# One result row per token and choice in an MoE kernel: written, not added, and summed on TensorE

## The chip, the cores and the metric

One core of a Trainium2 chip runs the whole program. The metric is device time in microseconds (us), the median of the runs shown. The engines are PE (TensorE, matmuls), DVE (VectorE), ACT (ScalarE), POOL (GpSimd) and SP (SyncE, which here issues transfers and does nothing else). "SPq" and "POOLq" in a row are the sequencers of these engines: issuing a transfer, waiting on a semaphore.

## What is computed

Two layers of a decoder step for 576 tokens of 1024 numbers (512 of a prompt, 64 of eight samples). Each layer is three kinds of sequence mixers behind one input projection, an output projection, a normalised residual, and then a mixture of 16 experts of which every token uses two, the two best of its best group of four. The part that this change touches, cut from the reference and put in short form:

```
h  = layer_norm-ed, modulated x            # [576, 1024]
e1, e2, w1, w2 = the two experts of a token, and their weights
y  = w1 * expert(e1, h) + w2 * expert(e2, h)
       # expert: silu(h @ W1) * (h @ W3) @ W2, 256 hidden
x  = layer_norm(ALPHA * x + gate * y)      # layer 0: goes on to layer 1's
                                           # projection; layer 1: the output
```

All of it is float32, and expert weights differ from layer to layer: 16 experts of three matrices of 1 MB each.

## The kernel before, in words

Tokens are five tiles of 128 rows, the fifth of 64 (the samples). The program runs through the mixers, the output projection with routing, the experts, and the combination of a layer; layer 0's combination feeds layer 1's input projection tile by tile.

**Rows.** The modulated input h of each token is stored by SP in a tensor hbuf in DRAM (L1633), one row for each token. Routing counts on the chip how many tokens each expert has and makes tables of row numbers. Blocks 0 to 15 are the experts in a fixed order; seven of the blocks (`LIGHT`) take 64 rows, the others up to 128, and further blocks stand in branches for experts with more tokens. Four left-over blocks, in a branch `nx > 0` (L2056) behind all others, are not needed with these inputs, so the branch is skipped.

**A block.** `gather` (L1314) is an indirect transfer that POOL issues: rows of hbuf by a column of the table. PE transposes them, `up` multiplies by W1 and W3 (float32 values in two parts for blocks of 128 rows), `hid` makes the hidden values, `down` multiplies by W2. ACT and DVE copy the result, times the token's weight, into a tile ys, of which there are two. `scatter` (L1379) is an indirect transfer by POOL that adds ys to rows of ybuf in DRAM. Two experts' scatters may add to the same row, so each waits until the one before it of another expert has landed; `declare_no_dep` lifts this only among the blocks of one expert. Nearly every scatter stands in the program twice, in the two sides of a branch `half` (for all rows, or for half of them), of which one is executed; `parts` returns the first of them. ybuf is zeroed in the mixers' time (L569).

**The order around it.** The loop over b is written out by hand: in its step b, PE goes from `up` of block b to `turn` of block b+1, POOL issues the gather of block b+2, then come `down` and `scatter` of block b-1. [...] SP loads the weights of three to four blocks ahead, 1 MB at a time, into three sets of buffers (wraw, slots, w3rd).

**The end of a layer.** Before the scatter of block 14, SP issues loads of ybuf for tiles 0 and 1 (`EARLY`, `take`, L1883). The results of blocks 14 and 15 reach these two tiles another way as well: `down` writes a second copy, times the gate g2 (L1368, DVE), into the tiles of gathered rows, and PE adds the right rows with a matrix of zeros and ones, `hot` (L2111, four matmuls of 128x512 for each tile). The scatters of blocks 14 and 15 are declared free of the EARLY loads, in their first variant (`st = parts(...)[0]`) and not in the second, which is the one executed here, so that one waits for these loads. Behind the branch of the left-over blocks SP loads the rows of tiles 4, 2 and 3. `combine` multiplies the rows by g2 (DVE, L2034 and L2096), adds them to x (L2098, L2122), and normalises: a reciprocal root in nine tiny DVE instructions (L353 to L359), then ACT, and the scale and shift by the rows of ln, on POOL (L2265 and L2266, or L2277 and L2284) and for the last tiles on DVE (L2279). In layer 0, a tile that is normalised is transposed by PE (L469), and layer 1's projection starts.

Of the kernel before, what the change touches and what calls it, by code (L numbers as in the profile page):

```python
# [44 lines left out]
THIRD = [b for b in range(NE) if RANK[b] < 2 + 2 * T // 257]  # L45
ORDER = (4, 0, 1, 2, 3)
# [15 lines left out]
def _tables():  # L62
# [47 lines left out]
    put("tok", np.stack([np.tile(p[:, None] - 127, (1, 5)), np.tile(128 * np.arange(5) - 896, (128, 1))], 2))  # L110

    put("off", 2046 + (p[:, None] >= 64))
# [43 lines left out]
def _body(nc, tc, a, ctx, dbg):  # L156
# [60 lines left out]
    hbuf = dp.tile([T, D], F32, name="hbuf")  # L217
    ybuf = dp.tile([T, D], F32, name="ybuf")
# [341 lines left out]
    def conv(l, S, hT, sp_):  # L560
# [6 lines left out]

        for t in ORDER:
            sp.dma_start(ybuf[tsl(t)], bz[:tp_(t)].rearrange("p g t -> p (g t)")[:, 0:D])  # L569
# [603 lines left out]
    def numbers(R, t, A):  # L1173

        n = tp_(t)
        for k in range(2):
            for i in range(2):
                dve.tensor_scalar(A[:, i, k], R["oh"][:n, t, i], R["w"][:n, t, i:i + 1] if k else R["tok"][:n, t, 0:1], None, op0=ALU.mult)
# [42 lines left out]
    def left_over(R, raw, tabs):  # L1221
# [14 lines left out]
        dve.tensor_tensor(tok[:, :, 0], *[C("tok").rearrange("p (t a) -> p t a", a=2)[:, :, i] for i in range(2)], op=ALU.add)  # L1236
# [32 lines left out]
        dve.tensor_scalar(tabs[0][:, c], ds, 1023.0, None, op0=ALU.add)  # L1269
# [29 lines left out]
    class Block:  # L1299
# [12 lines left out]
        def gather(self, r=None):  # L1312
            r = r or slice(0, self.rows)
            self.got = pool.indirect_dma_start(out=self.X[r], out_offset=None, in_=hbuf[:, :],  # L1314
                                    in_offset=bass.IndirectOffsetOnAxis(ap=self.tabs[0][r, self.col:self.col + 1], axis=0),
                                    bounds_check=T - 1, oob_is_err=False)
# [41 lines left out]
        def down(self, g=None, yg=None):  # L1358

            b, ys, wt = self.col, self.ys, self.tabs[1]  # L1360
            v = self.w[2].rearrange("p (f n) -> p f n", f=2)
            for h in range(2):
                c = slice(512 * h, 512 * (h + 1))
                p = ps(pl=self.pl)
                for f in range(2):
                    pe.matmul(p, self.hT[:, f], v[:, f, c], start=(f == 0), stop=(f == 1))  # L1366
                if yg is not None:
                    dve.scalar_tensor_tensor(yg[:, c], p, wt[:, b:b + 1], g[:, c], op0=ALU.mult, op1=ALU.mult)  # L1368
                if h == 0 or yg is not None:
                    act.activation(ys[:, c], p, AF.Copy, scale=wt[:, b:b + 1])  # L1370
                else:
                    dve.tensor_scalar(ys[:, c], p, wt[:, b:b + 1], None, op0=ALU.mult)

        def scatter(self, r=None):
            r = r or slice(0, self.rows)
            return self.add(ybuf[:, :], self.ys[r], self.to[r], T)

        def add(self, out, rows, to, n):
            st = pool.indirect_dma_start(out=out, in_=rows, in_offset=None,  # L1379
                                         out_offset=bass.IndirectOffsetOnAxis(ap=to, axis=0),  # L1380
                                         bounds_check=n - 1, oob_is_err=False, compute_op=ALU.add)
            for c, o in self.scat:
                if c % NE == self.col % NE and self.col < 3 * NE:
                    tc.declare_no_dep(st.ins, o.ins, reason="an expert's rows are distinct")
            self.scat.append((self.col, st))
            return st

    class Light(Block):
# [8 lines left out]
        def gather(self, r=None):  # L1397
            if not self.part:
                return super().gather(slice(0, 64))

            pool.indirect_dma_start(out=self.X[:, 0:512], out_offset=None, in_=hbuf[:, :].rearrange("t (h c) -> (t h) c", h=2),
                                    in_offset=bass.IndirectOffsetOnAxis(ap=self.tabs[3][:, 1, self.col:self.col + 1], axis=0),
                                    bounds_check=2 * T - 1, oob_is_err=False)
# [37 lines left out]
        def scatter(self, r=None):  # L1441
            return self.add(ybuf[:, :].rearrange("t (h c) -> (t h) c", h=2), self.ys[:, 0:512],
                            self.tabs[3][:, self.part, self.col:self.col + 1], 2 * T)
# [49 lines left out]
    def phase_b(l, gates, nrm, gst, slots, rqk, rv, x, R, tabs, rst, fill):  # L1493
# [123 lines left out]
        def experts_in(t):  # L1617
# [15 lines left out]
            sp.dma_start(hbuf[128 * t:128 * t + n], hps[t][:n].rearrange("q k p -> q (k p)"))  # L1633
# [51 lines left out]
        def ranked(t):  # L1685
# [3 lines left out]
            dve.tensor_tensor(An[:n, t, :, 0:2], bc(R["oh"][:n, t], 2, 2), bc(bc(C("tok")[:n, 2 * t:2 * t + 2], 1, 2), 3, 16), op=ALU.mult)  # L1689
# [26 lines left out]
        def finish(tq):  # L1716
# [9 lines left out]
            dve.tensor_scalar(srci[:, 0, 2:], pv[:, 0, 0, 2:], 1023.0, None, op0=ALU.add)  # L1726
            dve.tensor_scalar(srci[:, 1:3], pv[:, 1:3, 0], 1023.0, None, op0=ALU.add)
# [80 lines left out]
        dve.scalar_tensor_tensor(tabs[0][:, 0:2], pt[:, 384:386], 1023.0, tabs0, op0=ALU.add, op1=ALU.add)  # L1808
# [5 lines left out]
    def experts(last, finish, l, x, R, tabs, slots, rqk, rv, ahead):  # L1814
# [8 lines left out]
        with ExitStack() as sE:  # L1823
# [16 lines left out]
            def aside(b):  # L1840
# [10 lines left out]
                if b == NE - 2:  # L1851

                    o = _OFFS["iota256"][0]
                    src = lp.tile([128, 3, 2], F32, name="srcf", tag="ab", bufs=1)
# [3 lines left out]
                    dve.tensor_scalar(src[:, 1], src[:, 0], 256.0, 1024.0, op0=ALU.is_lt, op1=ALU.mult)  # L1858
                    dve.tensor_tensor(to, src[:, 0], src[:, 1], op=ALU.add)
                    for i in (1, 0):  # L1860
                        bl[NE - 2 + i].to = to[:ROWS[NE - 2 + i], i:i + 1]
                        dve.tensor_scalar(hot[:, 256 * i:256 * (i + 1)], hot[:, 0:256], src[:, 0, i:i + 1], None, op0=ALU.is_equal)
# [8 lines left out]
            def light(b, X, pl, part, y):  # L1871
                return Light(b, tabs, scat, X, xf[b % 2], hids[b % 2 if part == 0 else 2], y, sl if part == 0 else sl2, pl, part)
            bl = [light(b, Xs[b % 2], psp, 0, yss[b % 2]) if b in LIGHT else
                  Block(b, tabs, scat, Xs[b % 2], xs[b % 2], hids[b % 2], yss[b % 2], sl, psp, ROWS[b]) for b in range(NE)]

            gated = Xs[:2]
            hot = rv.rearrange("p t d -> p (t d)")
            bufs, loads = (slots[0][:, 0:D], slots[0][:, D:2 * D], slots[1][:, 0:D], slots[1][:, D:2 * D], slots[2][:, 0:D]), {}
            ys = dict(zip(CORDER, bufs))

            def take(t):

                loads[t] = sp.dma_start(ys[t][:tp_(t)], ybuf[tsl(t)])  # L1883
# [69 lines left out]
            for b in range(NE + 1):  # L1953
# [76 lines left out]
                if b > 0:  # L2030
                    if b == NE:
                        bl[b - 1].down(g2[:, 0], gated[1])
                        t = EARLY[0]
                        end = tc.keep_in_program_order(dve.tensor_tensor(ys[t], ys[t], g2[:, 0], op=ALU.mult))  # L2034
                    elif b == NE - 1:
                        bl[b - 1].down(g2[:, 0], gated[0])
                    else:
                        bl[b - 1].down()
# [4 lines left out]
                    if b > NE - 2:  # L2043
                        for t in EARLY:
                            tc.declare_no_dep(st.ins, loads[t].ins, reason="other rows")
# [10 lines left out]
            with tc.If(nx > 0), ExitStack() as sI:  # L2056
# [20 lines left out]
                t = EARLY[0]  # L2077
                dve.tensor_tensor(ys[t], ys[t], g2[:, 0], op=ALU.mult)
# [5 lines left out]
        return g2, ys, loads, take, gated  # L2084

    def combine(x, tail, rv, sG, leads):

        rp = mkpool(sG, "comb")
        g2, ys, loads, take, gated = tail
        hot = rv.rearrange("p t d -> p (t d)")  # L2090

        def pre(t):

            n, y = tp_(t), ys[t][:tp_(t)]
            if t != EARLY[0]:
                tc.keep_in_program_order(dve.tensor_tensor(y, y, g2[:n, int(t == 4)], op=ALU.mult))  # L2096
            if t in EARLY:
                dve.tensor_tensor(x[:, t], x[:, t], y, op=ALU.add)  # L2098

        def total(t):  # L2100

            n = tp_(t)
            xt, y = x[:n, t], ys[t][:n]
            st = rp.tile([128, 6], F32, name="cst", tag="cst", bufs=4)[:n]
            mu, var = st[:, 2:3], st[:, 3:4]
            if t in EARLY:
                bn = y[:, 0:12].rearrange("p (h a) -> p h a", h=2)
                for h in range(2):
                    c, p = slice(512 * h, 512 * (h + 1)), ps()
                    for i, r in ((1, gated[1]), (0, gated[0])):  # L2110
                        pe.matmul(p, hot[:, 256 * i + 128 * t:256 * i + 128 * (t + 1)], r[:, c], start=(i == 1), stop=(i == 0))  # L2111
                    if t == EARLY[0]:
                        dve.tensor_tensor(xt[:, c], xt[:, c], p, op=ALU.add)
                        dve.bn_stats(bn[:, h], xt[:, c])
                    else:
                        dve.scalar_tensor_tensor(xt[:, c], p, 1.0, xt[:, c], op0=ALU.mult, op1=ALU.add, accum_out=st[:, h:h + 1])
                if t == EARLY[0]:
                    dve.bn_aggr(st[:, 2:4], y[:, 0:12])
                    return st
                dve.tensor_scalar(mu, st[:, 0:1], st[:, 1:2], -1.0 / D, op0=ALU.add, op1=ALU.mult)  # L2120
            else:
                dve.scalar_tensor_tensor(xt, y, 1.0, xt, op0=ALU.mult, op1=ALU.add, accum_out=st[:, 0:1])  # L2122
                dve.tensor_scalar(mu, st[:, 0:1], -1.0 / D, None, op0=ALU.mult)  # L2123
# [17 lines left out]
        for t in CORDER:  # L2141
# [9 lines left out]
            yield t, mu, rstd, b, o, loads[CORDER[-1]]  # L2151
# [65 lines left out]
    for l in range(L):  # L2217
        with ExitStack() as sL:
# [22 lines left out]
            def norm_rows():  # L2241
                ln2 = [slots[:, D * i:D * (i + 1)] for i in (5, 0)]
# [115 lines left out]
```

## Time and profile before

| | |
|---|---|
| median of 3 runs | 1444.93 us (1441.07 to 1446.84) |
| the profiled execution | 1451.68 us, its span 1449.9 us |
| mean granted clock of PE | 0.91 |
| PE busy | 1206.7 us, 83% of the span |
| DVE, ACT, POOL busy | 830.8, 490.3, 444.5 us |
| experts of layer 0, of layer 1 | about 482 to 703 us, 1157 to 1403 us |
| POOL's transfers in all | 18.87 MB, 5.8% of 16 DMA engines |
| SP's transfers in all | 237.67 MB, 46.8% |

Times below are microseconds from the start of the span of the one execution that was profiled. In a timeline row the columns are start, duration, engine, line, operation, the tiles (out<-in), how many were joined into the row, and in brackets how long the engine was idle before it and what ended that. [...] A busy share of an engine is an average over stages with different limits, so it says little by itself; the waits do.

### The profile page before, as it was taken

The page shows a single profiled execution, that of the slowest core. Times are in us where ns is not written, and L with a number is a line of the kernel's source. Part 1 is how long each engine was busy: PE and PEld are TensorE (multiplying, and loading weights), DVE is VectorE, ACT ScalarE, POOL GpSimd, SP SyncE. Part 2 cuts the span into 40 slices and gives each one's busy share as a digit, 9 for nine tenths or more (in the row PEclk, how much of TensorE's full clock was granted, in tenths as well). Part 3 has the DMA queues.
Part 4 walks back from the last instruction along what each step waited for, and adds up shares of the span by engine and source line. Part 5 has one row for each costly group of instructions (what it writes and reads, how often), then busy time and mean ns, then how long its engine had stood idle before and what let it go on. Part 6 is the DMA issues. An engine that isn't in the chain of part 4 may idle for free. (4 is left out here: it accounts for less than half of the span.)

```text
span 1449.9 us, 22505 instructions
## 1 busy us (share of the span) xinstructions
PE 1206.7 (83%) x8086; PEld 922.8 (64%) x8086; DVE 830.8 (57%) x1903; ACT 490.3 (34%) x906; POOL 444.5 (31%) x354
## 2 busy tenths in 40 slices
PE   4999999998985688869679998999998578886980
PEld 0998677775774355557379977886676354455750
DVE  0577457446989431237786756736689833123567
ACT  0552133331343231326355313333135222222532
POOL 0014112215234553122151332232315355321215
PEclk8899999999987799969879998999998589898995
DMA  9545665855151648698444321026653173775942
GB/s 313 175 153 167 222 229 197 307 211 158 67 183 44 248 156 301 238 334 262 131 138 142 99 94 44 5 67 202 239 190 114 63 295 114 249 240 211 319 111 102
DMA packets 93135, 258.49 MB, mean 178 GB/s; under 512 B 25131, under 2 KB 53709, under 8 KB 74040
## 3 DMA queue, kind: packets, MB, share of 16 engines
q1 hardware_dynamic: 82136, 237.67, 46.8%
q0 software_dynamic: 10848, 18.87, 5.8%
q8 instruction: 86, 1.41, 0.4%
q14 instruction: 65, 0.53, 0.1%
HBM read 233.70 MB, written 34.70 MB: 185 GB/s over the span
## 5 line engine op out<-in xcount | busy, mean ns | idle before, releaser
L396 PE MATMUL ps<-whi,hT 128*128 128x256 f32 (+1 forms) x640 | 187.7, 293 | 0.8 <-DVE yi L712 0.8
L397 PE MATMUL ps<-wlo,hT 128*128 128x256 f32 (+1 forms) x640 | 182.6, 285 | 1.2 <-DVE wlo L323 1.2
L398 PE MATMUL ps<-whi,hT 128*128 128x256 f32 (+1 forms) x640 | 183.1, 286 | 0.1
L396 PEld LDWEIGHTS ps<-whi,hT 128*128 128x128 f32 (+1 forms) x640 | 116.8, 183 | 13.3 <-issue 10.3
L397 PEld LDWEIGHTS ps<-wlo,hT 128*128 128x128 f32 (+1 forms) x640 | 116.5, 182 | 4.1 <-issue 2.5
L398 PEld LDWEIGHTS ps<-whi,hT 128*128 128x128 f32 (+1 forms) x640 | 116.5, 182 | 2.3 <-issue 1.7
L386 PE MATMUL ps<-hT,whi 128*128 128x288 f32 x512 | 88.6, 295 | 0.0
L323 DVE TENSOR_TENSOR wlo<-wraw,whi 128x2048 fp32r<-128x2048 f32 x30 | 68.6, 2287 | 31.8 <-ACT whi L322 31.4
L323 DVE TENSOR_TENSOR wlo<-w3rd,whi 128x2048 fp32r<-128x2048 f32 x22 | 67.4, 3092 | 27.8 <-ACT whi L322 27.8
L1345 PE MATMUL ps<-whi,xh 128*128 128x256 f32 x384 | 62.1, 308 | 22.7 <-ACT whi L322 7.7
L1379 POOL DMA_INDIRECT ybuf<-ys,srci x20 | 32.6, 1632 | 141.0 <-DVEq L1985 36.8
L386 PEld LDWEIGHTS ps<-hT,whi 128*128 128x128 f32 x512 | 74.7, 188 | 0.4 <-ACT zdt L525 0.4
L259 PE MATMUL ada<-wada,scond 128*32 128x512 f32 x384 | 57.0, 665 | 19.4 <-DMA wada<-w_ada 19.4
L1558 PE MATMUL ps<-whi,mh 128*128 128x512 f32 (+1 forms) x160 | 68.8, 430 | 3.7 <-ACT mh L1544 3.7
L1345 PEld LDWEIGHTS ps<-whi,xh 128*128 128x128 f32 x384 | 54.5, 209 | 27.1 <-DVE xl L1333 9.0
L1560 PE MATMUL ps<-whi,ml 128*128 128x512 f32 (+1 forms) x160 | 66.5, 420 | 3.2 <-DVE ml L1545 3.2
L1366 PE MATMUL ps<-w3rd,hid 128*128 128x512 f32 x128 | 62.8, 635 | 5.5 <-ACT hid L1356 5.1
L1559 PE MATMUL ps<-wlo,mh 128*128 128x512 f32 (+1 forms) x160 | 67.3, 421 | 0.0
L1314 POOL DMA_INDIRECT qk<-hbuf,srci x32 | 33.8, 1057 | 95.5 <-PE ps L1413 43.3
L322 ACT ACTIVATE whi<-wraw 128x2048 fp32r<-128x2048 f32 x30 | 57.3, 1910 | 15.7 <-PE ps L386 7.6
L1345 PE MATMUL ps<-wlo,xh 128*128 128x256 f32 x384 | 57.0, 294 | 0.2 <-DVE wlo L323 0.2
L834 POOL TENSOR_TENSOR qh<-qx,ex 128x256 f32<-128x256 f32 x32 | 29.6, 953 | 89.4 <-issue 73.5
(544 smaller groups left out, 2864.9 us busy)
## 6 DMA issues: line engine op xcount, KB each, us to landing
wada<-w_ada SPq DMA_DIRECT2D x48, 1024.0 KB
wraw<-moe_w SPq DMA_DIRECT2D x36, 1024.0 KB
slots<-moe_w SPq DMA_DIRECT2D x30, 1024.0 KB
w3rd<-moe_w SPq DMA_DIRECT2D x30, 1024.0 KB
wraw<-w_in SPq DMA_DIRECT2D x22, 1024.0 KB
wraw<-w_out SPq DMA_DIRECT2D x8, 1024.0 KB
ybuf<-bz SPq DMA_DIRECT2D x8, 512.0 KB
slots<-ybuf SPq DMA_DIRECT2D x8, 512.0 KB
```

The source lines that it names most:

```text
L259: pe.matmul(acc[32 * q:32 * q + 32, :], sc_[:, k, :], w[:, o:o + 512], start=(k == 0), stop=(k == KD - 1))
L322: split.hi = act.activation(hi[:, :n], raw[:, :n], AF.Copy)
L323: dve.tensor_tensor(lo[:, :n], raw[:, :n], hi[:, :n].bitcast(F32), op=ALU.subtract)
L386: pe.matmul(p[:mw, :], lhs[:, k, m0:m0 + mw], rhs[:, k, 288 * h:288 * (h + 1)], start=(k == 0 and lhs is vh and rhs is hT[0]), stop=(k == ...
L396: pe.matmul(p[:n], hT[0][:, k, xs], vh[:, k, :], start=(k == 0), stop=False)
L397: pe.matmul(p[:n], hT[0][:, k, xs], vl[:, k, :], start=False, stop=False)
L398: pe.matmul(p[:n], hT[1][:, k, xs], vh[:, k, :], start=False, stop=(k == KD - 1))
L1345: pe.matmul(p, x[:, k], v[:, k], start=(x is self.xh and v is vh and k == 0), stop=(x is self.xl and k == KD - 1))
L1366: pe.matmul(p, self.hT[:, f], v[:, f, c], start=(f == 0), stop=(f == 1))
L1558: pe.matmul(p[:n], mh[:, k, :n], vh, start=(k == 0), stop=False)
L1559: pe.matmul(p[:n], mh[:, k, :n], vl, start=False, stop=False)
L1560: o = pe.matmul(p[:n], ml[:, k, :n], vh, start=False, stop=(k == 3))
```

## The change

- hbuf and ybuf have 1152 rows instead of 576: row t for a token's first choice and row 576 + t for its second. Every row of h is stored twice (L1633), and the tables hold the number of the row by choice.
- A scatter is a plain write. All scatters are declared independent of one another.
- Only tiles 0 and 1 of ybuf are zeroed, in both planes: four stores instead of five.
- Blocks 14 and 15 write their results as the other blocks do, ACT one half and DVE the other, into the tiles of gathered rows (`Xs`), which PE's `hot` matmuls read later; the gated copies (L1368) and the early product (L2034) are gone.
- A load of a tile of ybuf is two, one of each plane. Tiles 0 and 1 land in two weight buffers (wraw) that are free by then; tiles 4, 2 and 3 in slots. The rows of ln go into other places of slots in layer 0.
- `combine`: PE adds the two rows of a token with an identity matrix, and for tiles 0 and 1 the two `hot` products with them, in one accumulation per half of 512 columns: four matmuls a half instead of two for tiles 0 and 1, two instead of none for tiles 4, 2 and 3. DVE multiplies the sums by g2 from PSUM, half by half.

```diff
+PL, NONE = T, 2047
+NY = PL + T
...
-    hbuf = dp.tile([T, D], F32, name="hbuf")
-    ybuf = dp.tile([T, D], F32, name="ybuf")
+    hbuf = dp.tile([NY, D], F32, name="hbuf")
+    ybuf = dp.tile([NY, D], F32, name="ybuf")
...
-            sp.dma_start(hbuf[128 * t:128 * t + n], hps[t][:n].rearrange("q k p -> q (k p)"))
+            for o in (128 * t, PL + 128 * t):
+                sp.dma_start(hbuf[o:o + n], hps[t][:n].rearrange("q k p -> q (k p)"))
...
-        def add(self, out, rows, to, n):
+        def put(self, out, rows, to, n):
             st = pool.indirect_dma_start(out=out, in_=rows, in_offset=None,
                                          out_offset=bass.IndirectOffsetOnAxis(ap=to, axis=0),
-                                         bounds_check=n - 1, oob_is_err=False, compute_op=ALU.add)
-            for c, o in self.scat:
-                if c % NE == self.col % NE and self.col < 3 * NE:
-                    tc.declare_no_dep(st.ins, o.ins, reason="an expert's rows are distinct")
-            self.scat.append((self.col, st))
+                                         bounds_check=n - 1, oob_is_err=False)
+            for o in self.scat:
+                tc.declare_no_dep(st.ins, o.ins, reason="every choice of every token has its own row")
+            self.scat.append(st)
...
-                loads[t] = sp.dma_start(ys[t][:tp_(t)], ybuf[tsl(t)])
+                n = tp_(t)
+                if t not in ys:
+                    ys[t] = wraw.tile([128, 2048], F32, name="wraw", tag="raw").rearrange("p (k n) -> p k n", k=2)
+                loads[t] = [sp.dma_start(ys[t][:n, k], ybuf[PL * k + 128 * t:PL * k + 128 * t + n]) for k in range(2)]
...
         def pre(t):
-            n, y = tp_(t), ys[t][:tp_(t)]
-            if t != EARLY[0]:
-                tc.keep_in_program_order(dve.tensor_tensor(y, y, g2[:n, int(t == 4)], op=ALU.mult))
-            if t in EARLY:
-                dve.tensor_tensor(x[:, t], x[:, t], y, op=ALU.add)
+            n = tp_(t)
+            sums[t] = []
+            for h in range(2):
+                c, p = slice(512 * h, 512 * (h + 1)), ps()
+                rows = [(ident[:n, :n], ys[t][:n, k]) for k in range(2)]
+                if t in EARLY:
+                    rows += [(hot[:, 256 * i + 128 * t:256 * i + 128 * (t + 1)], kept[i]) for i in range(2)]
+                for i, (m, r) in enumerate(rows):
+                    pe.matmul(p[:n], m, r[:, c], start=(i == 0), stop=(i == len(rows) - 1))
+                sums[t].append(p)
...
         def total(t):
...
+            for h in range(2):
+                c = slice(512 * h, 512 * (h + 1))
+                tc.keep_in_program_order(dve.tensor_tensor(y[:, c], sums[t][h][:n], g2[:n, int(t == 4), c], op=ALU.mult))
...
-                ln2 = [slots[:, D * i:D * (i + 1)] for i in (5, 0)]
+                ln2 = [slots[:, D * i:D * (i + 1)] for i in (1, 3)]
```

The scheduler that orders each engine's instructions moves some of them with it. POOL's order at the end of the second layer's experts, before (`srcf` is the table of blocks 14 and 15, `srci` that of all blocks; L2056 is the branch of the left-over blocks):

```order
L1379 DMA ybuf<-ys_13035,srcf 576x1024
L1924 UNCONDITIONAL_BRANCH
L1924 REGISTER_ALU
L1924 COMPARE_AND_BRANCH
L1379 DMA ybuf<-ys_13036,srcf 576x1024
L1924 UNCONDITIONAL_BRANCH
L1916 TENSOR_LOAD ebi
L2056 COMPARE_AND_BRANCH
```

and in the changed kernel, from the last of the left-over blocks on:

```order
L2079 UNCONDITIONAL_BRANCH
L2061 UNCONDITIONAL_BRANCH
L2061 ISA
L2061 UNCONDITIONAL_BRANCH
L1935 REGISTER_ALU
L1935 COMPARE_AND_BRANCH
L1384 DMA ybuf<-qk,srcf 1152x1024
L1935 UNCONDITIONAL_BRANCH
L2280 TENSOR_TENSOR x<-x,ln_17069 128x1024
```

Block 15's scatter stood ahead of the branch and now stands behind it, in both layers. PE's order from block 15's `down` to the end of the program, before (L1366 is a matmul of `down`):

```order
L1366 MATMUL ps<-wraw,hid_13031 128x512 x2
L2111 MATMUL ps<-qk,v 128x512 x2
L1924 UNCONDITIONAL_BRANCH
L1916 TENSOR_LOAD ebi
L2056 COMPARE_AND_BRANCH
...
L2056 UNCONDITIONAL_BRANCH x2
L2111 MATMUL ps<-qk,v 128x512 x4
L2354 UNCONDITIONAL_BRANCH
```

and in the changed kernel (L1373 is the matmul of `down`, `cst` holds the identity, `qk` the kept results, `v` the matrices `hot`):

```order
L1373 MATMUL ps<-wraw,hid_13073 128x512 x4
L1935 UNCONDITIONAL_BRANCH
L1927 TENSOR_LOAD ebi
L2061 COMPARE_AND_BRANCH
...
L2061 UNCONDITIONAL_BRANCH x2
L2106 MATMUL ps<-wraw,cst 128x512
L2106 MATMUL ps<-qk,v 128x512 x2
L2106 MATMUL ps<-wraw,cst 128x512 x2
L2106 MATMUL ps<-slots,cst 64x512 x4
L2106 MATMUL ps<-slots,cst 128x512 x8
```

All of PE's sums now stand behind the branch: sixteen for tiles 0 and 1 in alternation of the two kinds, then four for each of tiles 4, 2 and 3. In the first layer it is the same, but the transposes of tile 0 stand between the sums of tile 4 and those of tile 2, where they stood ahead of all waits for the last loads before.

## Rows read from the trace of the kernel before

**Rows 1.** The page, 40 slices of 36 us: PE's granted clock in tenths.
```profile
PEclk8899999999987799969879998999998589898995
```

**Rows 2.** Busy time by stretches of 10 us, experts of the first layer.
```profile
core 0: us, PE busy (x) PEld busy (x) DVE busy (x) ACT busy (x) POOL busy (x), PEclk, DMA share, GB/s
620.00:630.00 10.00, 4.21 (x30) 4.00 (x28) 0.60 (x1) 0.00 (x0) 3.11 (x2) 0.84 1.02 394
630.00:640.00 10.00, 4.88 (x18) 2.44 (x18) 2.74 (x4) 2.35 (x5) 2.65 (x2) 0.57 1.00 350
```

**Rows 3.** The timeline (start, duration, idle before and what ended it), POOL, PE, ACT.
```profile
607.22 1.59 POOL L1379 DMA_INDIRECT ybuf<-ys,route  x1 [3.56 <-DMA ybuf<-ys,srci]
...
607.37 1.09 PE L1326 MATMUL ps<-cst,qk 128*128 128x128 f32 x8
...
618.36 3.68 POOL L1379 DMA_INDIRECT ybuf<-ys,route  x1 [9.55 <-ACTq L1974]
622.34 1.07 POOL L1314 DMA_INDIRECT qk<-hbuf,srci  x1 [0.30 <-issue]
...
634.38 0.69 ACT L1370 ACTIVATE ys<-ps,wslot 128x512 f32<-128x512 f32 x1 [17.05 <-DMA qk<-hbuf,srci]
...
635.12 1.97 PE L1326 MATMUL ps<-cst,qk 128*128 128x128 f32 x8 [10.90 <-ACT ys L1370]
```

**Rows 4.** Line L1379 from 607 us, then line L1314 from 622 us.
```profile
L1379 POOLq EVENT_SEMAPHORE  x1: 10583/10583/10583, 607.1 to 607.1; - x1
...
DMA to landing us min/median/max: 11.0/11.0/11.0
```

**Rows 5.** The waits of PE, 1160 to 1420 us (total, times, longest).
```profile
PE ps L1438 <- ACT ys L1370: 10.8, 1, 10.8
PE ps L1345 <- ACT whi L322: 4.9, 1, 4.9
PE ps L1326 <- DMA v<-hbuf,srci: 3.2, 1, 3.2
```

**Rows 6.** The timeline of POOL, the first gather of the first layer.
```profile
472.88 1.18 POOL L1314 DMA_INDIRECT qk<-hbuf,srci  x1 [6.74 <-DVE route L1143]
```

**Rows 7.** The timeline, the end of the second layer.
```profile
1397.79 16.85 SPq L1883 DMA_DIRECT2D slots<-ybuf  x5
...
1402.45 3.60 PE L2111 MATMUL ps<-qk,v 128*128 128x512 f32 x8
...
1403.20 1.43 POOL L1379 DMA_INDIRECT ybuf<-ys,srcf  x1 [9.90 <-ACT ys L1370]
...
1407.94 1.42 POOL L1379 DMA_INDIRECT ybuf<-ys,srcf  x1 [3.31 <-DMA ybuf<-ys,srcf]
...
1415.73 2.34 POOL L2284 TENSOR_TENSOR x<-x,ln 128x1024 f32<-128x1024 f32 x1
...
1416.83 2.32 DVE L2096 TENSOR_TENSOR slots<-slots 64x1024 f32<-64x1024 f32 x1 [1.71 <-DMA slots<-ybuf]
...
1422.38 1.22 DVE L2096 TENSOR_TENSOR slots<-slots 128x1024 f32<-128x1024 f32 x1
...
1424.96 2.10 DVE L358 SCALAR_TENSOR_TENSOR rq<-rq 64x1 f32<-64x1 f32 x1
```

**Rows 8.** The timeline, the end of the first layer's experts.
```profile
723.44 0.22 DVE L358 SCALAR_TENSOR_TENSOR rq<-rq 128x1 f32<-128x1 f32 x1
723.56 2.33 POOL L2265 TENSOR_TENSOR x<-x,slots 128x1024 f32<-128x1024 f32 x1 [11.94 <-ACT slots L2124]
...
723.70 2.22 DVE L359 SCALAR_TENSOR_TENSOR rq<-rq 128x1 f32<-128x1 f32 x1
...
725.95 2.38 DVE L358 SCALAR_TENSOR_TENSOR rq<-rq 128x1 f32<-128x1 f32 x1
...
730.10 1.97 PE L469 MATMUL ps<-cst,x 128*128 128x128 f32 x8 [16.59 <-ACT x L2257]
```

**Rows 9.** The groups by line, DVE: count | busy us, mean ns | idle before.
```profile
L1368 DVE SCALAR_TENSOR_TENSOR qk<-ps,wslot,slots 128x512 f32<-128x512 f32 x8 | 6.0, 748 | 6.3 <-PE ps L1366 6.3
```

More of the change, by code (lines that the diff above doesn't have):

```diff
@@ L108, in _tables @@
     put("pow2", np.tile(2.0 ** np.arange(16), (128, 1)))
-    put("tok", np.stack([np.tile(p[:, None] - 127, (1, 5)), np.tile(128 * np.arange(5) - 896, (128, 1))], 2))
-    put("off", 2046 + (p[:, None] >= 64))
+    rows = np.stack([np.tile((p - 127)[:, None, None], (1, 5, 2)),
+                     np.tile((128 * np.arange(5)[:, None] + PL * np.arange(2) + 127 - NONE)[None], (128, 1, 1))], 3)
+    put("tok", rows)
+    put("off", 2 * NONE + (p[:, None] >= 64))
     put("iota384", np.tile(np.arange(384.0), (128, 1)))
@@ L566, in conv @@
         pool.memset(bz, 0.0)
-        for t in ORDER:
-            sp.dma_start(ybuf[tsl(t)], bz[:tp_(t)].rearrange("p g t -> p (g t)")[:, 0:D])
+        for t in EARLY:
+            for k in range(2):
+                o = PL * k + 128 * t
+                sp.dma_start(ybuf[o:o + 128], bz.rearrange("p g t -> p (g t)")[:, 0:D])
         cw = cp_.tile([128, 6, 5], F32, name="cw")
@@ L1235, in left_over @@
         tok = R["tok"] = tl(NT, 2)
-        dve.tensor_tensor(tok[:, :, 0], *[C("tok").rearrange("p (t a) -> p t a", a=2)[:, :, i] for i in range(2)], op=ALU.add)
+        dve.tensor_tensor(tok, *[C("tok").rearrange("p (t k a) -> p t k a", k=2, a=2)[:, :, :, i] for i in range(2)], op=ALU.add)
         for t in ORDER:
@@ L2030, in experts @@
                 if b > 0:
[L2031 to L2038, printed above, removed]
+                    bl[b - 1].down()
                     if b == NE - 1:
@@ L2044, in experts @@
                         for t in EARLY:
-                            tc.declare_no_dep(st.ins, loads[t].ins, reason="other rows")
+                            for o in loads[t]:
+                                tc.declare_no_dep(st.ins, o.ins, reason="other rows")
                 if b == 0:
@@ L2083, in experts @@
                     take(t)
[L2084 removed]
+        return g2, ys, loads, kept
     def combine(x, tail, rv, sG, leads):
         rp = mkpool(sG, "comb")
[L2089 removed]
+        g2, ys, loads, kept = tail
         hot = rv.rearrange("p t d -> p (t d)")
+        sums = {}
         def pre(t):
[L2094 to L2098 removed]
+            n = tp_(t)
[8 more added lines that the diff above has]
+                sums[t].append(p)
@@ L2100, in total @@
         def total(t):
             n = tp_(t)
-            xt, y = x[:n, t], ys[t][:n]
+            xt, y = x[:n, t], ys[t][:n, 0]
             st = rp.tile([128, 6], F32, name="cst", tag="cst", bufs=4)[:n]
             mu, var = st[:, 2:3], st[:, 3:4]
[L2106 to L2116, printed above, removed]
-                if t == EARLY[0]:
[L2118 to L2123, printed above, removed]
@@ L2150, in combine @@
                 next(ahead, None)
-            yield t, mu, rstd, b, o, loads[CORDER[-1]]
+            yield t, mu, rstd, b, o, loads[CORDER[-1]][-1]
     def feat_ab(l, tp):
```

56 lines of the change are left out of this document (31 added, 25 removed).

## The prediction, made before the changed kernel ran

> **What bounds the kernel now.** I read the page's 40 slices first, then the waits of PE, then the timeline around the longest wait, and last the timeline at the end. [...]
>
> The longest wait of the first layer's experts is 10.90 us, from 624.2 to 635.1 us [rows 3]. Read it backwards. PE waits for ACT's ys, and ACT, idle for 17.05 us, for a gather of rows from hbuf. That gather left at 622.34 and landed 11.0 us later [rows 3, 4], at 633.3. It stood on POOL behind the scatter of 618.36, and this one behind a semaphore for 10.58 us [rows 4], from 607.1 to 617.7: the landing of the scatter of 607.22. It is the wait that adding into shared rows needs. Meanwhile the DMA engines were full, a share of 1.00 to 1.02 at 350 to 394 GB/s [rows 2].
>
> In the second layer PE's long waits are 10.8, 4.9 and 3.2 us [rows 5]. The end behind its last matmul is serial [rows 7]: scatter, landing, scatter, landing, the branch of the left-over blocks, the loads of tiles 4, 2 and 3, and then DVE from 1416.83 to the end.
>
> **The change part by part.** The profiled execution took 1451.68 us (span 1449.9); the median of the three runs is 1444.93. The sum is made against the execution, and the difference is then taken from the median.
>
> 1. Scatters write and are independent. Without the semaphore, the scatter of 618.36 can follow the one of 607.22 once that has been issued, at 607.22 + 1.59 = 608.8. The gather comes 622.34 - 618.36 = 4.0 us later, at 612.8, and lands at 612.8 + 11.0 = 623.8. ACT ran 1.0 us after the landing (634.38 against 633.3) and PE 0.7 after that, so PE goes on at 625.6 instead of 635.1: **-9.5**. Bounds: 0, if the landing grows by as much as the wait shrinks, and -10.9, the whole wait. I take -9.5, since the landing of 11.0 was already measured under full DMA engines. What is late next is a split of weights on ACT, which follows the same ys and moves with it.
>
> 2. The clock behind that wait. The same eight transposes take 1.97 us after it and 1.09 us before it [rows 3], and the clock of 630 to 640 was 0.57 with PE busy for 4.88 us [rows 2]. Without the idle time this stretch costs 4.88 x 0.57 = 2.8 us: **-2**; bounds 0 and -2.1.
>
> 3. The second layer's experts. The 10.8 us are a ys buffer that its own scatter has not left yet; a plain write must land too before the buffer is rewritten, so nothing is won. The 3.2 us wait is for a gather, and the 4.9 for a split that queues behind such a ys; both may shrink in part. Bounds 0 and -8.1; I take **-1**, nearer to nothing, as both sit behind landings that stay.
>
> 4. Experts' input stored twice. Five more stores of up to 0.5 MB a layer, beside the ones that are there. The first gather leaves POOL at 472.88, and what it waited for last, for 6.74 us, is DVE's table of rows [rows 6], not a store; the last tile's second copy must land within those 6.74 us: **0**. Bounds 0 and +1.3 a layer, one store of 0.5 MB at 394 GB/s [rows 2]. The zeroing, four stores instead of five, lies in the mixers beside other work: 0.
>
> 5. The end of the second layer. The loads for tiles 0 and 1 are four instead of two, 1 MB more, 2.7 us at 394 GB/s. Block 14's scatter in its executed variant waits for them, so it leaves at 1405.9 instead of 1403.20 [rows 7]. Behind it the two landings and the branch stand in series as before, in another order (block 15's scatter now goes behind the branch, and must land before the last loads): +2.7. Tile 4's rows are 0.26 MB more: +0.7. Their sum on PE is four matmuls of 128x512: L2111 shows 3.60 us for four (eight records, two for each) [rows 7], so **0.90** each and +3.6. DVE's product with g2 is then 0.75 per half from PSUM, the price of the like instruction L1368 [rows 9], one half beside PE and one behind it, in place of 2.32 [rows 7]: -1.6. Tiles 2 and 3 have two halves of 0.75 instead of one of 1.22 (1422.38) [rows 7]: +0.6. Sum **+6.0**. PE's sixteen matmuls for tiles 0 and 1, 14.4 us, run from 1405.9 to 1420.3, when tile 4's rows arrive; they hide beside the scatters and the loads. If that cover were gone, they would cost up to 14.4. [...]
> The 2.32 us product ran beside POOL's addition of 1415.73 to 1418.07 [rows 7], and so did DVE's tiny L358 beside a later one (2.10 us at 1424.96 [rows 7], 0.22 at 723.44 [rows 8]). [...]
>
> 6. The end of the first layer. The same +6.0 stands before PE's next matmul at 730.10, less two things that the shift takes along. POOL's additions began at 723.56 because their rows of ln were there; these now go into places that tile 4's and tile 2's rows hold until PE has summed them, so POOL begins later, and DVE's two tiny instructions of 2.22 and 2.38 us [rows 8] fall back to 0.2: -4.2. And PE is busy with sums until shortly before, so the projection does not begin at half clock: -1, half of step 2's figure. **+0.8**; bounds -4 and +8.
>
> DVE also loses four L1368 a layer, 0.75 us each [rows 9], beside PE's last expert matmuls, which set the time there: 0.
>
> Sum: -9.5 - 2 - 1 + 0 + 6.0 + 0.8 = **-5.7**, so 1446.0 for the execution and 1444.93 - 5.7 = **1439** for the median. A measurement of this kernel can tell about 0.5%, 7.2 us, from no change; this is within it.
>
> **The rivals.**
> *More than the named wait goes* (chance 0.23). Step 3 gives its 8.1 instead of 1, and the first layer's end its -4 instead of +0.8: -5.7 - 7.1 - 4.8 = -17.6, 1427. For it: scatters no longer hold up the gathers behind them on POOL, in either layer. Against it: the 4.9 and the 3.2 both hang on landings that stay [rows 5].
>
> *The DMA engines are the wait* (0.18). Between 620 and 640 us their share is 1.00 to 1.02 [rows 2]. Two scatters and a gather under way at once then share engines with the weights' loads, and each lands later by what the semaphore took before. Steps 1 to 3 give nothing: +6.8, 1452, and with step 4's bound for both layers 1454. [...] Against it: the rows that a scatter moves are 0.5 MB at most, 1.3 us at 394 GB/s.
>
> *PE's sums run at half clock* (0.13): slower. [...]
>
> *The change does not free the scatters* (0.04): each still waits for an earlier one on a semaphore that the two share, and for its ys buffer. [...]
>
> **How the numbers follow.** My own case has 0.42. Its spread is some 5 us, so about a third of it (0.15) is faster by over 0.5%. Faster: 0.15 + 0.23 = 0.38. Within 0.5%: 0.27 + half of the second rival (0.09) + 0.04 = 0.40. Slower: 0.09 + 0.13 = 0.22. The range reaches down to most of the first rival, 1425, and up to the second's bound and near the third, 1456.
>
> **What would show it.** In the profile after: no semaphore wait of 10 us before a scatter between 600 and 620, and a PE wait there of under 2 us (step 1); a clock of 1.0 behind it (step 2); block 14's last scatter 2.7 us later against the last expert's matmuls (step 5); PE's sums at 0.9 us and DVE's product at 0.75 (steps 5 and 6); L358 and L359 at 0.2 in the first layer's end. Wrong would be landings near 20 us, sums of 1.8 us, or a new wait of PE for hbuf at the first gather.

## The result and the profile after

| | before | after |
|---|---|---|
| median, same chip | 1445.88 us (4 runs) | 1462.22 us (4 runs) |
| ratio, 95% interval | | 1.0119 (1.0088 to 1.015) |
| profiled execution, its span | 1451.68, 1449.9 us | 1461.71, 1459.9 us |

The changed kernel is slower by 1.2%, 16 us. The forecast was 1439, its range 1425 to 1456: wrong, and on the other side. Yet the wait on which the forecast rested is gone. The page of the changed kernel, with the granted clock of the slices that answers to [rows 1], POOL's queue (q0), and the scatter's own line:

```profile
PE 1240.8 (85%) x8166; PEld 935.4 (64%) x8166; DVE 831.6 (57%) x1905; ACT 488.2 (33%) x902; POOL 422.8 (29%) x354
...
PEclk7999999999987799999989998999998599998997
...
q0 software_dynamic: 9952, 18.86, 3.7%
...
L1384 POOL DMA_INDIRECT ybuf<-ys,srci x20 | 21.0, 1051 | 163.9 <-DVE ys L1377 48.1
```

The same 18.86 MB go through POOL's queue, but the DMA engines need 3.7% of the span for them where adding took 5.8%, and a scatter's issue takes POOL 1.05 us where it took 1.63. POOL's timeline at the place of [rows 3, 4]:

```profile
595.34 1.03 POOL L1322 DMA_INDIRECT qk<-hbuf,srci  x1 [6.16 <-DMA ybuf<-ys,srci]
597.00 1.02 POOL L1384 DMA_INDIRECT ybuf<-ys,route  x1 [0.63 <-ACT ys L1443]
598.92 1.00 POOL L1384 DMA_INDIRECT ybuf<-ys,route  x1 [0.91 <-ACT hid L1364]
601.49 1.05 POOL L1322 DMA_INDIRECT qk<-hbuf,srci  x1 [1.57 <-PE ps L1334]
```

The second scatter follows the first after 1.9 us, and the gather that left at 622.34 leaves at 601.49. Of PE's waits in the first layer's experts (here 482 to 690 us) the longest, 10.9 us for ys, is gone and none stands in its place: the first of the three has its like before too (5.9 us), and the other two, the longest from 590 to 630 us, stood there before at the same length. PE's windows answer to [rows 2], with a clock of 0.83 and more where 0.57 stood, though not the 1.0 that the prediction named as its sign:

```profile
PE ps L1334 <- PEq L1996: 5.2, 1, 5.2
PE ps L1353 <- ACT xh L1340: 2.9, 1, 2.9
PE ps L1353 <- ACT whi L328: 2.8, 1, 2.8
```

```profile
610.00:620.00 10.00, 9.35 (x58) 7.56 (x57) 6.01 (x7) 2.36 (x6) 2.04 (x2) 0.85 1.01 420
620.00:630.00 10.00, 7.18 (x46) 6.77 (x46) 4.49 (x2) 4.83 (x5) 1.01 (x1) 0.83 1.02 421
```

So where did the time come from? The two programs load the same pieces of weights in the same order, each when a buffer behind PE's work is free, so the start of such a load shows how far PE is. From SP's timeline I take three: one at the end of the first layer's experts, one some 50 us into the second layer's mixers, one at their end. Before:

```profile
679.72 2.59 SPq L375 DMA_DIRECT2D w3rd<-w_in  x2
779.28 4.47 SPq L375 DMA_DIRECT2D wraw<-w_in  x2
1046.24 0.39 SPq L1529 DMA_DIRECT2D wraw<-w_out  x1
```

and after:

```profile
660.31 2.59 SPq L381 DMA_DIRECT2D w3rd<-w_in  x2
766.74 4.60 SPq L381 DMA_DIRECT2D wraw<-w_in  x2
1049.72 0.39 SPq L1533 DMA_DIRECT2D wraw<-w_out  x1
```

The changed kernel is 19.4 us ahead at the end of the first experts, 12.5 ahead at 779, and 3.5 **behind** at 1046. It loses 7 us at the first layer's end and 16 us in the second layer's mixers, a stretch that the diff does not touch. Of these 16, 15 lie behind the first load of w_out (897.60 us before, 886.03 after): there PE is idle for 9 us more, and its matmuls, of the same number within a few, take 6 us more at a lower clock (0.87 where it was 0.92, then 0.98 where it was 1.00).

How a program comes to change there can be read in the allocator. `ps` takes a PSUM tile (a place for PE's products, `ps` in the rows) from one of two pools by a counter of all calls:

```python
pl = psx if turns[0] % 7 > 4 and not held else psp
```

A combination calls it four times before and ten times after. All that is built behind the first layer's combination is handed tiles from the two pools in another phase, six steps on. PE's work in the second layer's mixers then stands in another order, though their code is the same; a run with the counter's step and no other edit has that order too (the phase alone, below). That the scheduler goes by the waits that come with a tile is the author's reading and was not shown.

### The profile page after: what moved, and what is told of

It reads as the page before. It is cut to its first block, busy times and chain, and to the rows that moved or that the text cites. A ratio compares the mean times of both kernels' runs of the same rounds, so it can differ in the third digit from the quotient of the medians.

```text
span 1459.9 us, 22701 instructions
## 1 busy us (share of the span) xinstructions
PE 1240.8 (85%) x8166; PEld 935.4 (64%) x8166; DVE 831.6 (57%) x1905; ACT 488.2 (33%) x902; POOL 422.8 (29%) x354
## 3 DMA queue, kind: packets, MB, share of 16 engines
q0 software_dynamic: 9952, 18.86, 3.7%
## 5 line engine op out<-in xcount | busy, mean ns | idle before, releaser
L1384 POOL DMA_INDIRECT ybuf<-ys,srci x20 | 21.0, 1051 | 163.9 <-DVE ys L1377 48.1
L1373 PE MATMUL ps<-w3rd,hid 128*128 128x512 f32 x128 | 59.8, 610 | 0.3
```

## The experiments

Each ran beside the kernel before on its chip. "Ahead" is read from the three loads above.

**The phase put back.** The changed kernel, with the counter moved one step more (6 + 1 = 7):

```diff
     for l in range(L):
+        if l:
+            turns[0] += 1
```

> The changed kernel with one line more: the counter by which ps() hands out PSUM tiles from one of two pools (its value modulo 7) is moved on by 1 ahead of layer 1. The change's sums take six more tiles in layer 0, so with this one it is seven, and layer 1's mixers get the pools, and PE gets the order there, that they had before the change. Theory: the whole loss of about 15 us between 876 and 1046 us of the profile is that shift; expected 1462 - 15 = 1447 us, and PE's lead of about 12 us at the start of layer 1's mixers still there at their end. Rival (something else that the change does slows the mixers, as the later POOL work or the transfers, and the order is worth nothing): 1462, within 3.

1450.52 against 1448.11, ratio 1.0018 (0.9994 to 1.0042), where the change had 1.0119: some 14 us come back by one line that computes nothing. SP's timeline:

```profile
661.43 2.59 SPq L381 DMA_DIRECT2D w3rd<-w_in  x2
765.60 4.60 SPq L381 DMA_DIRECT2D wraw<-w_in  x2
1035.07 0.39 SPq L1533 DMA_DIRECT2D wraw<-w_out  x1
```

18.3, 13.7 and 11.2 us ahead: up to 779 much as the changed kernel, and then most of the lead is kept. In the trace PE's weight loads of the second mixers, from about 750 to 1150 us, run in the order of the kernel before.

**The phase alone.** The kernel before, with `turns[0] += 6` in the same place.

> The kernel before with the same counter moved on by 6 ahead of layer 1, and nothing else. Theory: it loses what the changed kernel loses in layer 1's mixers, 15 us: 1461. Rival: as before, 1446, within 3.

1464.65 against 1448.11, ratio 1.011 (1.0087 to 1.0133). With no other edit this has the whole slowdown of the change, and PE's order in the second mixers is that of the changed kernel. In its waits of PE from 880 to 1050 us the same lines stand as before (first fence: before), longer and more of them:

```profile
PE ps L682 <- DVE P L677: 3.8, 1, 3.8
...
PE ps L884 <- ACT PT L879: 1.2, 2, 1.0
PE ps L1092 <- POOL slots L1090: 0.8, 3, 0.3
```

```profile
PE ps L682 <- DVE P L677: 4.6, 2, 3.3
PE ps L884 <- ACT PT L879: 3.1, 1, 3.1
PE ps L1092 <- POOL slots L1090: 2.2, 3, 1.5
PE ps L849 <- DVE kh L835: 1.6, 1, 1.6
```

The changed kernel's waits there are the same to 0.1 us (4.6, 3.1, 2.2 and 1.6). What moved shows in PE's order. At its first place of difference two pairs of small products change places around 48 matmuls of the input projection (sixteen times the three lines L396 to L398); first before, then this experiment:

```profile
871.85 1.06 PE L656 MATMUL ps<-cst,cv 128*128 128x128 f32 x4
...
881.19 0.61 PE L668 MATMUL ps<-cv,bz 128*128 128x128 f32 x4
```

```profile
867.29 1.17 PE L668 MATMUL ps<-cv,bz 128*128 128x128 f32 x4
...
876.49 0.60 PE L656 MATMUL ps<-cst,cv 128*128 128x128 f32 x4
```

The projection is work that PE does between the mixers' chains of small products. It is not used up sooner in the slow order: counted from about 745 us, when 700, 800 and 900 weight loads of the other products have run, those of the projection stand at 384, 432 and 576 in both, and at 1000 at 710 before and 696 here. What moves is the small products among themselves, and PE waits longer in their chains. Whether it is the other order or the tiles themselves that make these waits, and which piece makes how much of the loss, was not tried.

**Two other phases**, +2 and +4, again on the kernel before, to see whether six steps are a special case.

> The kernel before, with the counter of PSUM tiles moved two steps at the start of the second layer (the change moves it six). The compiled order of PE's second mixers differs in 160 rows, the fewest of the six steps. My theory: the phase of the kernel before is a good one among seven, and any other costs something: slower by 3 to 18 us, ratio 1.002 to 1.012. Rival: the +16 us belong to the six steps alone, and other phases fall on both sides of the kernel before: ratio 0.994 to 1.006, with no sign of its own.

> The same with four steps, whose order of PE's second mixers differs in 290 rows, the most. My theory: slower, and by more than with two steps if the number of moved rows counts: 5 to 20 us, ratio 1.003 to 1.014. Rival: as above, either sign, ratio 0.994 to 1.006; a version faster than 0.995 would be the phase to give the first layer's half of the change.

1461.14 and 1461.93 against 1446.35: ratios 1.0102 (1.0038 to 1.0166) and 1.0117 (1.0083 to 1.015). All three of the other phases that were tried cost 15 to 17 us, and the number of moved rows (160 for two steps, 290 for four) does not tell how much: the kernel before sits on a good phase. The steps 1, 3 and 5 were not tried, so that every other phase is worse is not shown; by the code an edit keeps this one where it adds a multiple of seven calls of `ps` ahead of the second layer.

The 16 us above come from one execution of each kernel. From the second of the three loads to the first load of the second layer's expert weights, nine executions in the phase of the kernel before (itself and the runs that keep it) took 278.2 to 285.6 us, the kernel before the shortest; the four in other phases took 290.5 to 297.0, the changed kernel 294.6. So it lost 9 to 16 us there; the medians, with the phase put back, say 14.

**The waits put back.** With the phase right, plain writes into own rows, but each scatter waits again for those of other experts:

```diff
-            for o in self.scat:
-                tc.declare_no_dep(st.ins, o.ins, reason="every choice of every token has its own row")
-            self.scat.append(st)
+            for c, o in self.scat:
+                if c % NE == self.col % NE and self.col < 3 * NE:
+                    tc.declare_no_dep(st.ins, o.ins, reason="an expert's rows are distinct")
+            self.scat.append((self.col, st))
```

> phase_back with the waits between scatters put back (independent only among the blocks of one expert, as before the change), the writes still plain. Theory (the wait was worth the gain of layer 0's experts, 21 us in the profile, of which 5 at 564 us may be another thing): 1447 + 16 = 1463. Rival (a plain write lands or issues faster than an adding one, and that was the gain): 1447.

1457.64, ratio 1.0063 (1.0043 to 1.0083): 7 us slower than with the phase put back, between the two expectations. POOL's timeline has the wait of [rows 3, 4] again, 8.71 us of idle time where it was 9.55, and PE waits 5.2 us behind it:

```profile
598.88 1.02 POOL L1384 DMA_INDIRECT ybuf<-ys,route  x1 [2.30 <-ACT ys L1444]
608.60 2.45 POOL L1384 DMA_INDIRECT ybuf<-ys,route  x1 [8.71 <-ACT xh L1340]
```

```profile
PE ps L1334 <- ACT ys L1375: 5.2, 1, 5.2
```

The independence is worth 7 us; with the plain write alone PE's wait is 5.2 us, where the adding scatters had 8.1 to 10.9 in five executions.

**Adding put back.** With the phase right, each choice its own row and the scatters independent, but adding as before (`compute_op=ALU.add`), into rows that are all zeroed (nine stores a layer instead of four).

> phase_back with scatters that add again, to rows of their own, all zeroed in the mixers, and still independent. Theory (the wait): 1447 for the 11 us stall, up to 1452 if the 5 us wait at 564 us needs the plain write. Rival (adding itself was slow): 1463.

1471.37, ratio 1.0167 (1.0145 to 1.019), 21 us slower than plain writes, and above both expectations. POOL's timeline:

```profile
606.02 1.59 POOL L1382 DMA_INDIRECT ybuf<-ys,route  x1 [0.61 <-ACT ys L1441]
609.62 1.57 POOL L1382 DMA_INDIRECT ybuf<-ys,route  x1 [2.01 <-ACT hid L1362]
611.50 1.07 POOL L1320 DMA_INDIRECT qk<-hbuf,srci  x1 [0.30 <-issue]
```

The long wait is gone here too, yet 1.6 us are back at each scatter, and the lead at the first experts' end is 6.6 us (673.11 against 679.72). Neither half of the change carries it alone, and the adding form pays the ends' costs as well. The five more zero stores a layer were not tried apart.

PE's time from about 470 us to the end of the first experts sets the halves side by side: 224.2 to 232.2 us in the five executions with the first layer of the kernel before, 222.7 with independent adding scatters, 217.3 with plain scatters that wait, and 209.9 to 215.1 in the six with both. So the plain write has the larger part in the gain.

**The ends.** Three edits on the kernel with the phase right. *Hot first*: PE's `hot` products for tiles 0 and 1, which need no load, go ahead of the identity products. *Both free*: the scatters of blocks 14 and 15 are declared free of the EARLY loads in the executed variant too, not in the first alone. *Ends*: both.

```diff
+            if t == EARLY[0]:
+                for u in EARLY:
+                    sums[u] = [ps(), ps()]
+                    for h in range(2):
+                        for i in range(2):
+                            pe.matmul(sums[u][h], hot[:, 256 * i + 128 * u:256 * i + 128 * (u + 1)], kept[i][:, 512 * h:512 * (h + 1)], start=(i == 0), stop=False)
...
-                    st = parts(b - 1, bl[b - 1].scatter, b - 1 in SSPLIT)[0]
+                    sts_ = parts(b - 1, bl[b - 1].scatter, b - 1 in SSPLIT)
```

> phase_back with PE's sums for tiles 0 and 1 in another order: the eight products with the matrices hot first (their operands are there when block 15 is done), then the eight with the identity, which need the loaded rows. Theory: PE's sixteen sums, and not the chain of scatters and loads, set the end of both layers: in phase_back PE stood idle for 4.0 us ahead of them, did the first four at up to 1.9 us each, and tile 4's rows waited for PE to reach them. Eight products in that idle time give back 5 to 7 us at the end of layer 1 and 3 to 4 of layer 0: 1450 - 9 = 1441. Rival (scatters and loads set the end, as the prediction had it): 1450, within 2.

> phase_back with the scatters of blocks 14 and 15 declared free of the loads of tiles 0 and 1 in both variants, and not in the first alone, so that block 14's no longer waits for their landing. Theory (PE's sums set the end): nothing, 1450 within 2, though the last loads are issued some 3 us earlier. Rival (the chain of scatters and loads): 3 us at each end, 1444.

> phase_back with both edits, the order of PE's sums and the freed scatters. With the sums no longer last, the chain of scatters and loads becomes the bound, and its 3 us count: 1441 - 4 = 1437, which would beat the kernel before (1448) by 0.7%. If the two do not add: 1441.

Against 1448.36: 1447.82, ratio 0.9998 (0.9976 to 1.0019); 1451.96, 1.0025 (1.0002 to 1.0049); 1449.43, 1.0015 (0.9994 to 1.0036). Hot first may be worth 2 or 3 us of the 9 expected (the intervals do not tell them from nothing), the freed scatters nothing, and the two do not add up. In its profile tile 4's sum with x does come 4.1 us sooner, counted from the start of the last expert's last matmuls (25.0 us where the phase put back had 29.1), but only 1.6 of these are left at the end of the span (58.2 against 59.8). Freed, block 14's scatter leaves 0.9 us after that start instead of 5.0, and the span ends no sooner (59.6 us): the forecast's chain, in which this scatter waits for the EARLY loads, is thus not what sets the end. What does set it, with PE's sums brought forward, stays open.

**One layer at a time.** The change in the first layer alone, with the counter's one step, and in the second alone, where none is needed; the other layer is that of the kernel before, its tables, adding scatters, blocks 14 and 15 and combination. In short form:

```diff
+NEW = (True, False)
...
+            if not NEW[LY[0]]:
+                return self.add(ybuf[0:T, :], self.ys[r], self.to[r], T)
...
-                pre(t)
+                (pre if new else pre_old)(t)
```

> The change in the first layer alone, with the counter of PSUM tiles moved one step at the second layer's start, so that its mixers are handed the tiles of the kernel before; the second layer's tables, scatters, blocks 14 and 15 and combination are those of the kernel before (adding, chained, gated copies). My theory: the first layer's plain, independent scatters win 21 us of PE's time by its last experts, its own end gives 5 to 8 back, and the second layer's end, which cost 8.8, is no longer paid: PE's matmuls at the second layer's first expert some 11 us ahead of the kernel before, and still so at the end: about 1437 beside 1448, a ratio of 0.990 to 0.995. Rival 1: the lead is lost in the second layer in any case, because its experts wait for weights and landings at their own times (lead at the end under 4 us): a ratio of 0.997 to 1.000. Rival 2: the mixers' order is moved by something else than the counter: slower than the kernel before.

> The complement: the first layer as in the kernel before, the change in the second layer alone; the counter needs no step, as the first layer's combination takes four tiles as before. My theory: nothing is won up to the second layer's experts, 3 us are won in them, and the second layer's end costs 8.8: about +6, 1454 beside 1448, a ratio of 1.003 to 1.006. Rival: the second layer's end costs less when PE comes to it later, as its loads have landed by then: no difference, 0.998 to 1.001.

Against 1447.20: 1444.57, ratio 0.9991 (0.9967 to 1.0014), and 1455.48, 1.0058 (1.0033 to 1.0083). The second layer costs 8 us, about as expected; the first brings 3 and not 11, which is its first rival's range and no more than can be told from nothing. No version here beats the kernel before by more than the noise.

Why not 11? The second run is a control for the first: its first layer is the kernel before's. There PE waits for ys 8.6 us, not 10.9:

```profile
PE ps L1342 <- ACT ys L1385: 8.6, 1, 8.6
```

and with the phases +2, +4 and +6, which leave the first layer alone too, 8.4, 8.1 and 8.9 us. The execution from which the forecast read 10.9 was 5.8 us above its kernel's median here (1451.68 against 1445.88) and had the longest wait of five. It also came late to the first of the three loads: three of four others with the same first layer came there at 671.8 to 676.2 us instead of 679.72 (the fourth, at 679.85, was 6.3 us late already at 470), and against these three the leads above are 4 to 8 us too large. From 470 us to the end of the first experts, by PE's matmuls, the adding first layer of this control took 6.3 us less than in that execution, and the plain one of the first run 17.1 less: the difference, some 11 us, is the gain. At the layer's end 6 of them go back, which leaves 5 beside the 3 measured.

## Why the prediction was wrong

**The step that failed** is one that "The change part by part" does not have. It asks what each edited instruction costs, and nothing of what the ten calls of `ps` do to those built behind them. It has no term for the stretch from 760 to 1160 us; some 14 us were lost there. The orders that it goes by are those around the edits; the order of the whole program would have shown moved rows in mixers that the diff leaves alone, though not their price. No rival held this case either. Without it (the phase put back) the ratio is 1.0018, +2.6 us against the forecast's -5.7, inside the range.

**Steps 1 and 2** were right in that the wait and the half clock went, and nearly right in size, the latter in part by luck. Forecast -11.5; against executions of the same chip some -11. But step 1 gave the whole gain to the independence, and with that alone (adding put back) the first experts took 222.7 us, little less than the 224.2 to 232.2 before; the larger part came with the plain write, to which the forecast gave nothing. One place where it shows: the scatter at 552.50 landed 11.1 us after its issue, the same one in the changed kernel 4.9 us, and PE's 5.1 us wait for `hid` behind it is gone. That the adding alone does this is not shown: of the other executions with adding scatters, four have a wait for `hid` of 4.0 to 5.1 us in these experts (before_phase, before_phase_2, second_only, adds), but before_phase_4 has none among its seven longest, of which the last is 1.8 us. The bound "the landing grows by as much as the wait shrinks" did not come true: at a DMA share of 1.00 to 1.02 the two scatters of 597.00 and 598.92 landed after 10.6 us each and the gather behind them after 11.2.

**Step 3** forecast -1: from 1165 us to the last expert the changed kernel gains 2.7 us on the kernel before by PE's matmuls. **Step 4** forecast nothing, and holds: the first gather leaves at 474.81 instead of 472.88, but PE was 1.5 us late already at 415, and the gather waits for the same table as long as before [rows 6], 6.74 us.

**Step 5** forecast +6.0. Tile 4's sum with x starts at 1419.25 before and at 1429.21 after, +10.0; PE was 2.4 late at the last expert, so the end costs **+7.6**. Block 14's scatter left 1.2 us later against the last expert's last matmuls (5.5 us behind their start, 4.3 before), not 2.7. The rows of this end, the last two with the columns of [rows 2]:

```profile
1406.78 0.92 POOL L1384 DMA_INDIRECT ybuf<-qk,srcf  x1 [11.33 <-SPq L2061]
...
1408.87 3.40 PE L2106 MATMUL ps<-wraw,cst 128*128 128x512 f32 x4 [3.87 <-SPq L2061]
1412.11 1.88 PE L2106 MATMUL ps<-qk,v 128*128 128x512 f32 x4
...
1423.42 2.35 POOL L2280 TENSOR_TENSOR x<-x,ln 128x1024 f32<-128x1024 f32 x1 [8.76 <-ACT x L2279]
1424.22 10.71 PE L2106 MATMUL ps<-slots,cst 64*64 64x512 f32 x24
1424.32 0.69 DVE L2118 TENSOR_TENSOR wraw<-ps,slots 128x512 f32<-128x512 f32 x1 [1.73 <-PE ps L2106]
1425.12 1.73 DVE L2125 SCALAR_TENSOR_TENSOR x<-wraw,x 128x1024 f32<-128x1024 f32 x1
...
1429.21 1.22 DVE L2125 SCALAR_TENSOR_TENSOR x<-slots,x 64x1024 f32<-64x1024 f32 x1
...
1408.87:1412.20 3.33, 3.33 (x5) 1.54 (x6) 0.00 (x0) 0.00 (x0) 0.00 (x0) 0.57 0.50 154
1412.20:1416.00 3.80, 3.80 (x11) 1.65 (x10) 1.84 (x3) 0.00 (x0) 0.90 (x1) 1.00 0.02 5
```

Two prices held: 0.94 us for a matmul (four records, 1.88, are two) against 0.90, and 0.69 for the half product against 0.75. The cover failed. PE waits 3.87 us, by the profile for SP's sequencer and not for a scatter, starts at 1408.87 and not at 1405.9, and its first four records take 3.40 us at a granted clock of 0.57, the next four 1.88 us at 1.00: the third rival, for two matmuls and not for all. Sums that all run at half clock, the case near which the range's upper end was set, no run shows. The sums of tiles 0 and 1 end at 1424.2, and tile 4's follow with no wait for rows, so PE comes last here, as "if that cover were gone" had it. That PE alone sets the end is not shown: with its sums brought forward (hot first) little was won.

POOL works in SBUF from 1423.42 to 1425.77. Beside it, L2118, which reads one operand from PSUM and one from SBUF, keeps its 0.69 us, and L2125, with two in SBUF, takes 1.73 where the same line takes 1.23 without a neighbour (at 700.12, below). That a product from PSUM keeps its price beside POOL, as step 5 has it, no row of the prediction shows; it was the author's estimate, and with 0.69 us here the price of 0.75 was the right choice. A row was there before, too: L2116, which reads PSUM, took 0.69 us at 1413.55 beside POOL's L2277. And it is not always DVE that pays: at 1433.41 L2125 began 0.04 us ahead of POOL's L2280 and kept 1.23, and POOL's took 3.38 us where the one at 1423.42 took 2.35.

**Step 6** forecast +0.8 and cost 6 to 7 us: from the first of the three loads to the second six executions with the change's first layer took 104.2 to 107.6 us, five with that of the kernel before 98.3 to 99.6. The waits of PE and the timeline of the first layer's end, which answer to [rows 8]:

```profile
PE ps L402 <- ACT hT L493: 7.0, 1, 7.0
PE ps L475 <- ACT x L2260: 3.9, 2, 3.1
```

```profile
700.12 1.23 DVE L2125 SCALAR_TENSOR_TENSOR x<-wraw,x 128x1024 f32<-128x1024 f32 x1
...
710.47 1.09 PE L475 MATMUL ps<-cst,x 128*128 128x128 f32 x8 [3.14 <-ACT x L2260]
710.49 5.73 POOL L2268 TENSOR_TENSOR x<-x,slots 128x1024 f32<-128x1024 f32 x2 [18.81 <-ACT x L2260]
710.51 3.44 DVE L2125 SCALAR_TENSOR_TENSOR x<-slots,x 128x1024 f32<-128x1024 f32 x1
...
716.27 2.29 DVE L365 SCALAR_TENSOR_TENSOR cst<-rq 64x1 f32<-64x1 f32 x1
718.59 2.27 DVE L2151 TENSOR_TENSOR cst<-cst 64x1 f32<-64x1 f32 x1
```

Up to the second tile's transposes the step is right: 730.10 - 702.73 = 27.4 us from the last expert's end before, 710.47 - 683.22 = 27.3 after, and the 16.6 us wait is spread under the sums. POOL's additions begin later, as said. But the -4.2 is no saving: they now fall beside DVE's work on tiles 2 and 4, where L2125 takes 3.44 us (1.23 at 700.12), L365 2.29 (0.16 at 696.60) and L2151 2.27, against the prediction's sign of 0.2 for such instructions, and PE then waits 7.0 us for a tile's hT. The forecast moved the contention away and did not ask what it would stand beside next.

In sum, with the phase right: -11 and -3 for the experts, +6 and +8 for the ends, about 0, and +2.6 measured. So beside the missing term, step 6 is the one that was mis-sized most.

## What to carry to other kernels

Before pricing an edit, compare the compiled order of the whole program, not of the edited place: a counter that later code shares can move work hundreds of microseconds away, and here that cost more than any term of the sum. Then put the shared state back by hand (one line that computes nothing) and time the edit again, or its effect and the accident's are one number. And read a wait that carries a forecast from several executions: this one was 10.9 us in the one at hand, and 8.1 to 8.9 in four others. So it is with a loss: the 16 us of one pair are 9 to 16 against nine executions.

## What was not expected of the hardware

An indirect write that adds was dearer here than a plain one even with nothing to wait for: 1.63 us of POOL's time against 1.05 for each (means of twenty), and 5.8% of the DMA engines' span against 3.7% for the same 18.9 MB. It goes with the form: with adding put back the scatters from 540 to 625 us take 1.57 to 1.63 us, but for one of 2.46, where the plain ones of the changed kernel take 1.00 to 1.04, but for one of 1.83; and with the plain form in the first layer alone the share is 4.8%. One landing was 11.1 us against 4.9, for the scatter at 552 us; elsewhere the landings are alike (10.4 us at 541.19 before and 10.2 at 540.51 after, 9.6 at 592.15 and 9.5 at 585.08). With adding put back, and the zeroing that it needs, the kernel was 21 us slower.
